# Loads of attention keys and queries issued by SyncE in place of GpSimd

## The chip, the cores and the metric

One core of a Trainium2 chip runs the whole program in one launch. The metric is the device time of one execution in microseconds (us). The engines are TensorE (PE, with its weight loads as PEld), VectorE (DVE), ScalarE (ACT), GpSimd (POOL) and SyncE (SP), each with its own queue of instructions, taken in order. A DMA is issued by an instruction in one of these queues and then runs on the core's 16 DMA engines.

## What is computed

The reference runs two transformer blocks over 1024 tokens of width 1024, in float32. The first has window attention, spatial gating, attention to a memory and a mixture of experts. The second has a recurrent unit beside a differential attention, and then experts that choose their tokens. The change lies in the differential attention of the second block: four heads, each with two sets of queries and keys of 64 channels and values of 128 channels.

```python
def diff_attention(q, k, v, g_q, g_k, lam, g_o, bias_table, lam_init):
    q = rms_norm_2(q, g_q) * (HEAD_DK ** -0.5)
    k = rms_norm_2(k, g_k)
    ...
    def block(args):
        ...
        s = jnp.einsum('bqhjd,bkhjd->bhjqk', qi, k).astype(jnp.float32) + bias[None, :, None]
        p = jax.nn.softmax(s, axis=-1)
        w = (p[:, :, 0] - lam * p[:, :, 1]).astype(v.dtype)
        return jnp.einsum('bhqk,bkhd->bqhd', w, v)
    ...
    o = rms_norm_2(o, g_o) * (1.0 - lam_init)
    return o.reshape(B, S, D_ATT)

def second_block(...):
    ...
        y_att = diff_attention(...)
        mix = jnp.dot(jnp.concatenate([y_lru, y_att], axis=-1), w_out[l])
        x = x + gate1 * mix
        h2 = rms_norm_2(x, g_norm2[l]) * (1.0 + scale2) + shift2
        x = x + gate2 * expert_choice_ffn(h2, w_router[l], w1[l], w3[l], w2[l])
```

## The kernel before

Matrix products work on pairs of tiles: an upper part (12 bits of the significand) and a lower part of each number, so that a product is made of several passes. Queries and keys are normed, split into both parts, transposed and stored in DRAM as `qT_d` and `kT_d`. Of the 128 rows of a tile there, 64 hold the upper parts of a head's 64 channels and 64 the lower ones.

`head_load` brings a head into nine SBUF tiles of 128 partitions by 1024 float32 numbers (512 KB each), with the tag `hd`. For each of the two sets there is a query tile `q` (upper rows on partitions 0 to 63, lower ones on 64 to 127) and two key tiles: `kh`, the upper key rows twice over the partitions, and `kl`, the lower key rows twice. Two strips `st` from `F_d` hold the position bias, and one tile holds the values from `v_d`. In the kernel before, queries (L2068) and keys (L2072) are issued from the GpSimd queue. The key load reads 64 rows through an access pattern whose outermost dimension repeats them twice. Strips (L2078) and values (L2084) are issued from the SyncE queue. There are slots for two heads (18 tiles of class `hd`).

For each head and each of 8 tiles of 128 queries, `diff_att` makes the scores of both sets on the PE (`diff_half`, L2108 with `kh` and L2109 with `kl`, into the PSUM tile `p_sc`), adds the bias and takes the minimum on DVE (L2115), takes exponents on ACT (L2098), combines the two sets (L2145 on DVE, or L2148 on ACT with L2150 on GpSimd), transposes the weights on the PE (L312, `p_wt`), copies them (L315 on ACT or L317 on DVE), multiplies them with the values (L2159, `p_o`), and norms the result with a power on GpSimd (L2166), after which it is transposed once more (L2175, `p_ot`).

The order on every queue is written when the program is built, by a list scheduler (`Sched`): generators yield pieces of work with an engine and an estimated cost, and the scheduler puts each at the end of its engine's queue in the order of the estimated times. A transfer is estimated on a virtual engine called DMA or, if GpSimd issues it, on POOL. Each engine then takes its queue in order, and an instruction waits by semaphores for the data and the buffers that it needs. A tile's buffer is one of 48 (`u`), taken over from some earlier tile, whose last reader must be done.

Around the head loads the same queues hold: on SyncE the stores of the values (`v_d<-v`), the output weights (`wraw<-in_w_out`, L369), the rows `gmod`, `grow` and `mscale`, and the other half of the mixed features (`yl<-ylru_d`); on GpSimd the products of the output weights with a gate row (L379, `wraw<-wraw,grow`).

After the attention come the output projection with the router (`out2`), the choice of each expert's tokens (`top_part`, `route2`) and 16 experts (`expert2`), whose weights stream from DRAM.

Of the kernel before, what the change touches and what calls it, by code (L numbers as in the profile page):

```python
# [37 lines left out]
# ---------------------------------------------------------------- order of the work  # L38

class Ev:  # L40
    """Something that a generator makes and others wait for."""
# [6 lines left out]
class Sched:  # L48
    """Puts the work of generators in one order for the engines' queues.

    A generator yields, before each piece of work, the engine that it keeps and an estimate of its
    time; the order is that of a list schedule by these estimates."""
# [17 lines left out]
    def spawn(self, prio, gen, at=0.0):  # L70
        g = [prio, self.n, gen, at, at, None, 0.0]   # prio, id, gen, ready, last, request, slots ready
        self.n += 1
        self.gens.append(g)
        cur = getattr(self, "cur", None)
        self._next(g, None)
        self.cur = cur
        return g
# [8 lines left out]
    # requests  # L86
# [9 lines left out]
    def give(self, cls, t=None, n=1):  # L96
        """Slots of a class back, from the end of the caller's last piece of work."""
# [87 lines left out]
# ---------------------------------------------------------------- pieces  # L185
# [26 lines left out]
def bcast_rows(ap, n, p=128):  # L212
    """A row of n values of DRAM on p partitions."""
    return bass.AP(tensor=ap.tensor, offset=ap.offset, ap=[[0, p], [1, n]])


class K:
# [15 lines left out]
    # pieces of generators  # L233
    def load(self, out, src, mb, eng=None):
        """A transfer of mb megabytes into out."""
# [7 lines left out]
    def split(self, hi, lo, src, n):  # L243
        """hi = the upper 12 bits of src's significand, lo = the rest."""
# [6 lines left out]
    def rstd(self, ss, n, mul=1.0):  # L251
        """mul / sqrt(ss / n + eps); mul is a power of two."""
        nc, S = self.nc, self.S
        w = ss.shape[1]
# [8 lines left out]
    def transposes(self, name, parts, outs, n=128):  # L263
        """Up to four [128, 128] blocks through one bank, then its upper and lower parts."""
# [12 lines left out]
    def tsplit(self, name, groups, view=lambda p: p):  # L277
        """Blocks transposed to both parts: groups of (parts, upper, lower, time from which the parts are there)."""
# [22 lines left out]
    def tcopy(self, name, groups, view=lambda p: p):  # L301
        """Blocks transposed: groups of (parts, output, time from which the parts are there)."""
# [23 lines left out]
    def gemm(self, out, hT, ch, n, whole=False):  # L326
        """out [128 tokens, n] = h @ W from upper and lower parts; hT(k) gives those of h."""
# [17 lines left out]
    def wload(self, chunks):  # L345
        """Streams chunks (weights, first column, columns, uses) of [K, columns] as both parts."""
        S, nc = self.S, self.nc
        pool = 0
        for n, ch in enumerate(chunks):
# [6 lines left out]
            if isinstance(ch, tuple):  # L356
                # these after what the gpsimd queue has by then
# [35 lines left out]
    def wdone(self, ch, i):  # L393
        """A user has read a piece of a chunk."""
# [4 lines left out]
    def short(self):  # L399
        """A small vector instruction, and the wait for what it wrote."""  # L400
        return self.S.op("DVE", 0.085, lat=0.01)
# [17 lines left out]
def staggered(pairs):  # L419
    """Each expert's last weights after the next expert's first ones."""  # L420
# [16 lines left out]
def gain_tile(k, name, src, n=1024):  # L437
    """A gain on all partitions."""
# [5 lines left out]
# ---------------------------------------------------------------- first block: mixers  # L444
# [23 lines left out]
def sgu_prep(k, ev):  # L468
    """Masked, transposed mixing weights [j, g, i] in both parts and the bias [i, g]."""
# [51 lines left out]
def sgu_mix(k, ghl, prep_ev, dones, s_ev):  # L521
    """s[t] = mixed gate + bias, token-major."""
# [50 lines left out]
def att_kv(k, t, hT, ch, gk, kT, vhl, done):  # L573
    """Keys: both parts, each twice over the partitions; values."""
# [35 lines left out]
def att_q(k, t, hT, ch, out_ev):  # L610
    """Normed queries, both parts on the partitions: [part * 64 + d, head, token]."""
# [32 lines left out]
def att_half(k, t, g, qT, at, kT, vhl, mask, nsink, sink, ev):  # L644
    """Four heads of a token tile: at[:, 4g:4g+4]."""
# [90 lines left out]
def out1(k, t, hT, chs, x_in, x1_d, gate, stored):  # L736
    """x1 = x + mixed @ w_out to DRAM."""
# [30 lines left out]
def proj_res(k, t, n, hT, ch, x_ev, done):  # L768
    """x[:, half n] += h @ W."""
# [26 lines left out]
def cross_norm(k, t, gate, x1_d, gain_ev, out_ev):  # L796
    """The norm of x1, transposed."""
# [155 lines left out]
def out_cross(k, t, o_ev, chs, x1_d, x2_d, h_d, gain_ev, wr_ev, lg, done, stored):  # L953
    """x2 = x1 + o @ w_co; it and its norm to DRAM; router logits."""
# [62 lines left out]
def first_mixers(k, x_in, x1_d, x2_d, h_d, sg_d, lg, moe=True, more=()):  # L1017
# [6 lines left out]
    # constants  # L1024
# [36 lines left out]
    def body():  # L1061
        """Everything in the order of its priority."""
# [18 lines left out]
        # spatial gating  # L1081
# [20 lines left out]
        # window attention  # L1102
# [40 lines left out]
        # memory  # L1143
# [60 lines left out]
        def load_wr():  # L1204
# [6 lines left out]
            # the norm's gain, by channel  # L1211
# [57 lines left out]
def grow(k, dones, tab):  # L1269
    """More slots for the experts' weights as the tokens' are given back."""  # L1270
# [12 lines left out]
def first_max(k, x, w, oh, mx, t):  # L1283
    """mx = max of x [128, w]; oh = 1 at its first place."""
# [11 lines left out]
def route_tile(k, t, lg, lgd, prev, done, gdone):  # L1296
    """Group and experts of a tile's tokens; their places in the table of the experts' slots."""
# [58 lines left out]
def route_gate(k, t, G, ohg, mg, m, c1, OH, lh, rh, gdone):  # L1356
    """Gates of both experts, with the group's weight."""
# [34 lines left out]
def tokens(k, tok, ids, q):  # L1392
    """Rows to gather; that of an empty slot is past every array."""
# [24 lines left out]
def route1_rest(k, dones, ev):  # L1418
    """Blocks of 128 past the first of each expert: where they start, and their slots."""
# [26 lines left out]
    # a slot of a first block is in no column  # L1446
# [30 lines left out]
def rest_place(k, evs, stop, cont):  # L1477
    """Stops the order of the work where the loop over the further blocks stands."""
# [13 lines left out]
def moe1_start(k, dones):  # L1492
    """Tiles that the tokens' rows are gathered into: empty slots keep what was there."""
# [80 lines left out]
def moe1_consts(k):  # L1574
# [5 lines left out]
    # tri[i, j] = 1 where i < j  # L1580
# [21 lines left out]
def moe1_rest(k, a, h_d, x_d):  # L1602
    """Experts with more than 128 tokens: their further blocks, one at a time."""
    nc, tc, cp = k.nc, k.tc, k.cp
    # expert of block j: the number of experts whose blocks end at or before j
# [62 lines left out]
# ---------------------------------------------------------------- second block  # L1668

def mod_vec(k, mod_d, ev):  # L1670
    """silu(c) @ w_mod + b_mod as a row in DRAM."""
# [38 lines left out]
def mod_gain(k, ev, gate, mod_d, j, g):  # L1710
    """g * (1 + scale) on all partitions."""
# [20 lines left out]
def second_norm(k, t, gate, x_d, g_ev, s_ev, hT2, out_ev):  # L1732
    """h1 transposed."""
# [971 lines left out]
```

## Time and profile before

| What | Value |
|---|---|
| median of 3 runs | 2645.89 us |
| lowest and highest run | 2645.14 and 2654.83 us |
| profiled execution, first to last instruction (its span) | 2648.8 us |
| profiled execution, time around its span | not shown |
| PE busy | 2403.0 us (91%) |
| DVE busy | 1961.7 us (74%) |
| ACT busy | 1574.9 us (59%) |
| GpSimd busy | 503.1 us (19%) |
| moved by DMA | 600.76 MB, 227 GB/s over the span |

Busy shares are averages over the whole span; stages differ, and what a change in one stage is worth is read from that stage. Times in the rows are counted from the span's start. The profile does not count the issue of a DMA as busy time of an engine.

### The profile page before, as it was taken

What the parts mean: (1) busy time and instruction counts of PE and PEld (TensorE: products, weight loads), DVE (VectorE), ACT (ScalarE), POOL (GpSimd) and SP (SyncE); (2) the same over time, 40 slices, a digit from 0 to 9 for tenths busy, and PEclk for the clock granted to TensorE, in tenths of its full rate; (3) what the DMA queues carried; (4) which work ended last, traced back from release to release, by engine and by line L of the source; (5) the groups of instructions that cost most, each with busy time, mean ns of one, the idle gap of its engine ahead of it and who ended that gap; (6) DMA issues with size and microseconds to landing.
All of it is one profiled execution on the core that took longest, in us unless ns stands there. A gap on an engine that the chain in (4) does not pass through costs nothing. (4 is left out here: it accounts for less than half of the span.)

```text
span 2648.8 us, 34944 instructions
## 1 busy us (share of the span) xinstructions
PE 2403.0 (91%) x11984; PEld 1975.1 (75%) x11984; DVE 1961.7 (74%) x3174; ACT 1574.9 (59%) x2419; POOL 503.1 (19%) x407
## 2 busy tenths in 40 slices
PE   7999999999698999999969998976894799999998
PEld 6887877888577877777747777765783688877776
DVE  6668457555788888888865546667829799899897
ACT  5357235442276877777864667655622577677775
POOL 1021011000321132111122202234435000110110
PEclk9999999999899999999979999988997899999999
DMA  4433465134688999999972213654326699999998
GB/s 152 149 111 124 166 232 203 47 112 152 205 271 290 344 302 322 348 341 345 350 263 81 79 53 108 154 115 112 103 104 246 225 359 358 380 374 373 375 373 270
DMA packets 328660, 600.76 MB, mean 227 GB/s; under 512 B 47176, under 2 KB 78476, under 8 KB 328480
## 3 DMA queue, kind: packets, MB, share of 16 engines
q1 hardware_dynamic: 296224, 550.15, 59.1%
q0 software_dynamic: 32256, 48.35, 7.6%
q8 instruction: 95, 1.56, 0.3%
q14 instruction: 85, 0.70, 0.1%
HBM read 554.25 MB, written 60.87 MB: 232 GB/s over the span
## 5 line engine op out<-in xcount | busy, mean ns | idle before, releaser
L389 DVE TENSOR_TENSOR wl<-wraw,wh 128x1024 fp32r<-128x1024 f32 x829 | 990.1, 1237 | 132.6 <-ACT wh L384 124.8
L384 ACT ACTIVATE wh<-wraw 128x1024 fp32r<-128x1024 f32 x852 | 846.0, 1051 | 90.7 <-DMA wraw<-in_w_ck_dram 34.8
L260 POOL TENSOR_TENSOR rs_r<-rs_v,mhalf 128x1 f32<-128x1 f32 (+2 forms) x111 | 103.7, 937 | 786.4 <-DVE rs_v L257 786.3
L340 PE MATMUL p_b<-wl,xT_h 128*128 128x512 f32 x512 | 203.0, 397 | 9.1 <-DVE wl L389 9.1
L340 PE MATMUL p_a<-wl,xT_h 128*128 128x512 f32 x512 | 204.4, 399 | 6.3 <-DVE wl L389 6.0
L339 PE MATMUL p_b<-wh,xT_h 128*128 128x512 f32 x512 | 205.3, 401 | 1.6 <-ACT wh L384 1.6
L339 PE MATMUL p_a<-wh,xT_h 128*128 128x512 f32 x512 | 206.2, 403 | 0.0
L341 PE MATMUL p_a<-wh,xT_l 128*128 128x512 f32 x512 | 201.5, 394 | 0.2 <-DVE xT_l L249 0.2
L341 PE MATMUL p_b<-wh,xT_l 128*128 128x512 f32 x512 | 201.0, 393 | 0.0
L339 PE MATMUL p_g<-wh,aT_h 128*128 128x512 f32 x384 | 157.5, 410 | 0.0
L341 PE MATMUL p_g<-wh,aT_l 128*128 128x512 f32 x384 | 150.8, 393 | 0.0
L340 PE MATMUL p_g<-wl,aT_h 128*128 128x512 f32 x384 | 150.7, 392 | 0.0
L1559 POOL DMA_INDIRECT x_d<-y,tok x32 | 60.0, 1873 | 351.7 <-ACT y L1550 348.0
L340 PEld LDWEIGHTS p_a<-wl,xT_h 128*128 128x128 f32 x512 | 97.1, 190 | 37.4 <-DVE wl L389 19.1
L2399 POOL DMA_INDIRECT out_dram<-y,tok x16 | 38.0, 2378 | 452.7 <-DVE y L2389 347.7
L340 PEld LDWEIGHTS p_b<-wl,xT_h 128*128 128x128 f32 x512 | 96.7, 189 | 35.6 <-DVE wl L389 16.9
L247 ACT ACTIVATE xT_h<-p_t 128x512 fp32r<-128x512 f32 x96 | 56.8, 596 | 95.8 <-PE p_t L269 95.3
L339 PEld LDWEIGHTS p_b<-wh,xT_h 128*128 128x128 f32 x512 | 96.8, 189 | 21.1 <-ACT wh L384 1.9
L341 PEld LDWEIGHTS p_a<-wh,xT_l 128*128 128x128 f32 x512 | 96.8, 189 | 20.2 <-DVE xT_l L249 0.6
L339 PEld LDWEIGHTS p_a<-wh,xT_h 128*128 128x128 f32 x512 | 97.2, 190 | 19.1
L341 PEld LDWEIGHTS p_b<-wh,xT_l 128*128 128x128 f32 x512 | 96.5, 188 | 19.8
L339 PE MATMUL p_y<-wh,hidT 128*128 128x512 f32 x256 | 103.6, 405 | 6.1 <-SPq L1624 6.1
(502 smaller groups left out, 5826.5 us busy)
## 6 DMA issues: line engine op xcount, KB each, us to landing
wraw<-in_w_dram SPq DMA_DIRECT2D x768, 512.0 KB
mraw<-in_w_mod_dram SPq DMA_DIRECT2D x48, 512.0 KB
x<-x_d SPq DMA_DIRECT2D x32, 512.0 KB
wraw<-in_w_in_dram SPq DMA_DIRECT2D x28, 512.0 KB
wraw<-in_w_out_dram SPq DMA_DIRECT2D x16, 512.0 KB
hd<-kT_d POOLq DMA_DIRECT2D x16, 512.0 KB, 20.2
x<-in_x_dram SPq DMA_DIRECT2D x8, 512.0 KB
xres<-in_x_dram SPq DMA_DIRECT2D x8, 512.0 KB
```

What stands on the lines that cost most here:

```text
L247: nc.scalar.activation(hi, src, AF.Copy)
L260: nc.gpsimd.tensor_tensor(r, v, self.mhalf[:, :w], op=OP.pow)
L339: nc.tensor.matmul(out, hh(k), wh, start=(k == 0), stop=False)
L340: nc.tensor.matmul(out, hh(k), wl, start=False, stop=False)
L341: nc.tensor.matmul(out, hl(k), wh, start=False, stop=(k == KK - 1))
L384: nc.scalar.activation(hi, raw, AF.Copy)
L389: (nc.vector if S.chosen == "DVE" else nc.gpsimd).tensor_tensor(lo, raw, f(hi), op=OP.subtract)
L1559: nc.gpsimd.indirect_dma_start(out=x_d, out_offset=bass.IndirectOffsetOnAxis(ap=k.tok[:, e:e + 1], axis=0), in_=y, in_offset=None, compute ...
L2399: nc.gpsimd.indirect_dma_start(out=out, out_offset=bass.IndirectOffsetOnAxis(ap=k.tok2[:, e:e + 1], axis=0), in_=y, in_offset=None, comput ...
```

## The change

Queries and keys are issued from the SyncE queue. A key tile is loaded by two transfers, one for each half of the partitions, both from the same 64 rows, in place of one that repeats the rows. The destination is viewed as plain float32 (`f(q)`, `f(kt)`). The scheduler's estimates change with it: 1.0 on POOL for each load becomes 1.5 on DMA for a query tile and 0.75 on DMA for half a key tile. The rest of the difference takes out comments and docstrings.

```diff
@@ -2064,17 +2064,17 @@
     for b in range(2):
         g = 2 * h + b
         q, kh, kl = hd[3 * b:3 * b + 3]
-        yield S.op("POOL", 1.0, after=[t0])
-        nc.gpsimd.dma_start(q, qT_d[g])
+        yield S.op("DMA", 1.5, after=[t0])
+        nc.sync.dma_start(f(q), qT_d[g])
         for kt, r in ((kh, 0), (kl, 64)):
-            src = kT_d[g, r:r + 64]
-            yield S.op("POOL", 1.0, after=[t0])
-            nc.gpsimd.dma_start(kt, bass.AP(tensor=src.tensor, offset=src.offset, ap=[[0, 2], [1024, 64], [1, 1024]]))
+            for o in (0, 64):
+                yield S.op("DMA", 0.75, after=[t0])
+                nc.sync.dma_start(f(kt)[o:o + 64], kT_d[g, r:r + 64])
         T["q", b], T["kh", b], T["kl", b] = q, kh, kl
```

The order of the instructions changes in the attention stage on all engines; behind it only buffer numbers differ on the PE. Two places matter for what follows.

The first is SyncE's queue where the third head (head 2) is loaded. `hd_16185` to `hd_16187` before, and `hd_16174` to `hd_16182` in the change, are its tiles. Before:

```order
L2084 DMA hd_15240<-v_d 128x1024
L2084 DMA hd_15454<-v_d 128x1024
L2078 DMA hd_16185<-F_d 128x1024
L2078 DMA hd_16186<-F_d 128x1024
L2084 DMA hd_16187<-v_d 128x1024
L369 DMA wraw<-in_w_out_dram 128x2x512 x2
L237 DMA gmod<-in_g_norm_2_dram 128x1024
```

With the change:

```order
L2084 DMA hd_15458<-v_d 128x1024
L2068 DMA hd_16174<-qT_d 128x1024
L2072 DMA hd_16175<-kT_d 64x1024 x2
L2072 DMA hd_16176<-kT_d 64x1024 x2
L2068 DMA hd_16177<-qT_d 128x1024
L2072 DMA hd_16178<-kT_d 64x1024 x2
L2072 DMA hd_16179<-kT_d 64x1024 x2
L2078 DMA hd_16180<-F_d 128x1024
L2078 DMA hd_16181<-F_d 128x1024
L2084 DMA hd_16182<-v_d 128x1024
L369 DMA wraw<-in_w_out_dram 128x2x512 x2
L2068 DMA hd_16721<-qT_d 128x1024
```

The ten loads of queries and half keys now stand between the last load of head 1 and the strips of head 2; head 3's loads (from `hd_16721`) follow the two loads of output weights, ahead of `gmod`.

The second is GpSimd's queue where the first products L379 stand. `r` is the power of a tile, `s` the sum of its two sets, `hd` tiles are head 3's. Before:

```order
L2166 TENSOR_TENSOR r_16779<-v_16778,mhalf 128x1
L2150 TENSOR_TENSOR s_16460<-s_16460,s_16461 128x512
L2072 DMA hd_16721<-kT_d 128x1x1024
L2068 DMA hd_16722<-qT_d 128x1024
L379 TENSOR_TENSOR wraw<-wraw,grow 128x1024 x4
L2166 TENSOR_TENSOR r_16863<-v_16862,mhalf 128x1
L2166 TENSOR_TENSOR r_16928<-v_16927,mhalf 128x1
L2072 DMA hd_16723<-kT_d 128x1x1024
```

With the change:

```order
L2166 TENSOR_TENSOR r_17026<-v_17025,mhalf 128x1
L379 TENSOR_TENSOR wraw<-wraw,grow 128x1024 x2
L2166 TENSOR_TENSOR r_17090<-v_17089,mhalf 128x1
L2150 TENSOR_TENSOR s_16668<-s_16668,s_16669 128x512
...
L2166 TENSOR_TENSOR r_17364<-v_17363,mhalf 128x1
L2150 TENSOR_TENSOR s_16981<-s_16981,s_16982 128x512
L379 TENSOR_TENSOR wraw<-wraw,grow 128x1024 x2
L2166 TENSOR_TENSOR r_17451<-v_17450,mhalf 128x1
```

The issues of loads are gone from this queue, and the four products stand in two pairs: one late among head 2's tiles, one among head 3's.

## Rows read from the trace of the kernel before

**Rows 1.** Span of the core and mean granted TensorE clock.

```profile
core 0: 2648.8 us, clock 0.959
```

**Rows 2.** Stretches: from:to, length; busy us (instructions) by engine; PEclk, DMA share, GB/s.

```profile
core 0: us, PE busy (x) PEld busy (x) DVE busy (x) ACT busy (x) POOL busy (x), PEclk, DMA share, GB/s
1720.00:1755.00 35.00, 34.63 (x244) 30.91 (x242) 34.80 (x121) 31.24 (x71) 18.09 (x21) 1.00 0.54 115
1755.00:1783.00 28.00, 9.85 (x32) 7.46 (x33) 5.94 (x21) 4.65 (x11) 3.14 (x4) 0.57 0.64 142
1783.00:1803.00 20.00, 20.00 (x142) 18.07 (x141) 18.05 (x62) 17.32 (x40) 10.46 (x13) 1.00 0.28 84
...
1813.00:1832.00 19.00, 15.30 (x95) 13.03 (x95) 18.96 (x56) 16.17 (x34) 7.04 (x8) 0.91 0.46 128
1832.00:1852.00 20.00, 8.45 (x36) 6.83 (x35) 7.05 (x19) 4.06 (x8) 1.83 (x3) 0.66 0.29 84
1852.00:1884.00 32.00, 31.12 (x216) 27.08 (x214) 29.75 (x101) 29.43 (x64) 11.40 (x12) 1.00 0.16 50
1884.00:1902.00 18.00, 12.85 (x93) 11.79 (x94) 10.00 (x23) 9.28 (x25) 7.46 (x7) 0.91 0.75 250
1905.00:2010.00 105.00, 100.94 (x528) 84.31 (x528) 52.01 (x101) 32.26 (x47) 45.52 (x24) 1.00 0.29 105
...
2075.00:2645.00 570.00, 559.50 (x2543) 452.48 (x2541) 511.36 (x500) 412.23 (x469) 56.86 (x29) 1.00 1.01 355
```

**Rows 3.** PE in order of time: start, us, instruction, [idle before <-releaser].

```profile
1680.01 0.39 PE L2108 MATMUL p_sc<-hd,hd 128*128 128x512 f32 x1
...
1760.86 0.77 PE L2108 MATMUL p_sc<-hd,hd 128*128 128x512 f32 x1 [5.93 <-DMA hd<-kT_d]
1771.19 0.80 PE L2109 MATMUL p_sc<-hd,hd 128*128 128x512 f32 x1 [9.56 <-DMA hd<-kT_d]
...
1842.07 0.77 PE L2108 MATMUL p_sc<-hd,hd 128*128 128x512 f32 x1 [9.68 <-DMA hd<-kT_d]
```

**Rows 4.** GpSimd in order of time, 1640 to 1920.

```profile
1649.84 0.61 POOL L2068 DMA_DIRECT2D hd<-qT_d  x1 [12.43 <-DMA qT_d<-qkT]
...
1734.50 0.63 POOL L2068 DMA_DIRECT2D hd<-qT_d  x1
...
1744.19 1.62 POOL L2072 DMA_DIRECT2D hd<-kT_d  x2
...
1803.42 9.25 POOL L379 TENSOR_TENSOR wraw<-wraw,grow 128x1024 f32<-128x1024 f32 x4
...
1828.77 0.84 POOL L2072 DMA_DIRECT2D hd<-kT_d  x1
```

**Rows 5.** SyncE's issues in order of time, 1600 to 1960.

```profile
1672.68 8.52 SPq L241 DMA_DIRECT2D v_d<-v  x3
...
1692.24 0.79 SPq L2084 DMA_DIRECT2D hd<-v_d  x2
1719.18 1.00 SPq L2078 DMA_DIRECT2D hd<-F_d  x2
...
1805.27 9.74 SPq L2078 DMA_DIRECT2D hd<-F_d  x2
...
1827.79 25.63 SPq L237 DMA_DIRECT2D yl<-ylru_d  x4
```

**Rows 6.** Line L2072, the key loads: from issue to landing.

```profile
DMA to landing us min/median/max: 15.9/20.2/31.3
```

**Rows 7.** DMA queues from 1836 to 1842, then 1720 to 1725: packets, MB, share of 16 engines.

```profile
q0 software_dynamic: 238, 0.43, 21.4%
...
q1 hardware_dynamic: 384, 1.44, 93.2%
```

**Rows 8.** DVE in order of time, 1798 to 1818.

```profile
1802.60 10.63 DVE L2145 SCALAR_TENSOR_TENSOR s<-s,c,s 128x512 f32<-128x512 f32 x1
```

**Rows 9.** DVE's groups, 1680 to 1902: busy us, mean ns | idle before.

```profile
L2145 DVE SCALAR_TENSOR_TENSOR s<-s,c,s 128x512 f32<-128x512 f32 x32 | 33.8, 1064 | 0.0
L317 DVE COPY wT<-p_wt 128x512 f32<-128x512 f32 x19 | 12.9, 682 | 1.2 <-PE p_wt L312 1.2
```

## Prediction

> **What bounds the kernel now.** I read the page first, then the table of stages, then the waits and the order in time of the attention stage. The page's busy shares are averages over stages with different limits; the change touches one stage, the attention of the second block, from about 1680 to 1902 us. The table of stages [rows 2] shows what the reader must see there. From 1720 to 1755 DVE is busy 34.80 of 35 us and the PE 34.63: the two engines together set the pace of a head, about 37.5 us (two heads' scores from 1680.01 [rows 3] to 1755). Then come two holes. From 1755 to 1783 DVE works 5.94 us of 28, from 1832 to 1852 it works 7.05 of 20, and the PE's granted clock falls to 0.57 and 0.66, near its 1.2 GHz level, after the engine had stood still. The PE in order of time says what ended the holes [rows 3]: 5.93 and 9.56 us before the first scores of head 2, and 9.68 us before a score of head 3, all waiting for `hd<-kT_d`, a key tile. Head 0 has no such wait: its first score, at 1680.01, carries no idle time before it, and the stretch to 1755 has none worth the name.
>
> Why are the keys late? GpSimd issues head 2's first query load at 1734.50 and its last pair of keys at 1744.19 [rows 4], while SyncE had issued the same head's bias strips at 1719.18 [rows 5]. So buffers were free some 15 us earlier; the loads stood in the GpSimd queue behind the additions L2150 and the powers L2166. Head 3's last key load leaves at 1828.77, behind the four products of L379, which take 9.25 us [rows 4]. And a key load is slow once issued: 15.9, 20.2 and 31.3 us to landing (least, median, most) [rows 6]. While hardly anything but two key loads is in flight, from 1836 to 1842 us, the GpSimd queue keeps 21.4% of the 16 DMA engines busy and moves 0.43 MB in 6 us, 72 GB/s; SyncE's strips and values move 1.44 MB in 5 us, 288 GB/s [rows 7]. 21.4% of 16 is 3.4 engines, so under two for each of the transfers.
>
> The Trainium skill, page "DMA: Bandwidth & Descriptors", section "Rules for kernel authors", says that a leading zero-stride broadcast of c copies holds a DMA to at most c engines; the old key load has c = 2, and the trace agrees (3.4 engines for two).
>
> **The change part by part.**
> *Removed from GpSimd:* 24 issues, 0.63 us for a query tile and 0.81 to 0.84 us for a key tile [rows 4], some 18 us. GpSimd is busy 18.09 of 35 us where the stage is full [rows 2], so I count nothing for it; what it hides behind are the scores on PE and DVE.
> *Added on SyncE:* 8 query loads and 32 half key loads, 0.4 to 0.5 us of issue each by the rows of the strips and values, where two take 1.00 and 0.79 us [rows 5], so 16 to 20 us in all. SyncE waits most of this stage. Cost: nothing, as long as nothing urgent stands behind a waiting load.
> *When the loads start.* The first group of order rows shows head 2's ten loads directly behind head 1's last one. By the program's semaphores its keys and queries wait for nothing later than the last score of head 0, and its strips and values for products a few tiles behind. The strips' issue at 1719.18 [rows 5] is the row nearest to that; ten issues from there end by about 1725. Head 3's loads follow behind two loads of output weights; their buffers come free from the end of head 1 (about 1755) to a third of the way into head 2.
> *How long they take.* A head is nine tiles of 0.524 MB, 4.72 MB. At 288 GB/s that is 16.4 us. No row shows a transfer of 64 partitions, so I bound it: not faster than 288 GB/s, and not slower than the old key loads' 72 GB/s. I take 288, the row of the same queue with the same 4 KB runs. Head 2 is then there by 1742, and its scores are wanted at 1755; head 3, if all nine tiles had to wait until 1768, by 1785, wanted at 1755 + 37.5 = 1792. Head 0 (from 1650, as on GpSimd now [rows 4]) is there by 1667, wanted at 1680. Head 1's loads stand behind the last store of values, issued by 1681.2, and most of them behind a wait for those stores to land, which ended at 1692.24 [rows 5]: there by 1709, wanted at 1680 + 37.5 = 1717.
>
> The page "SBUF — State Buffer" of the Trainium skill, section "Can I just issue two DMAs to hit both halves?", speaks against the halves: only a transfer over all 128 partitions reaches all ports, and two halves run one after the other. By it (an estimate) the keys would move at half of 288 GB/s, 14.6 us for 2.1 MB, and a head would take 23.7 us instead of 16.4; no run here shows it, and head 0 would still be there by 1674.
>
> *The sum.* The two holes: 28 + 20 = 48 us, in which 12.99 us of DVE work is done. In the four full stretches (1720 to 1755, 1783 to 1803, 1813 to 1832, 1852 to 1884) DVE is idle 4.44 of 106 us, 4.2% [rows 2], so that work takes 13.6 us without the wait: 34.4 us are freed. The slow clock after each hole is inside this figure.
> The scheduler also moves five copies of transposed weights (L317) from ACT to DVE: 5 x 0.68 us [rows 9] = 3.4 us, with DVE the bound.
> The products of L379 hold DVE: one L2145 ran from 1802.60 for 10.63 us while they ran [rows 8], against 0.75 us for the other 31 ((33.8 - 10.63) / 31) [rows 9]. The second group of order rows shows them split in two pairs. Bounds: the pairs hold DVE as the four did (no difference), or not at all (9.9 us gained). I take the first, since the same instruction still runs beside them.
> Saving: 34.4 - 3.4 = 31.0 us. What follows the stage (output projection to 2010, choice of tokens to 2075, experts to 2645) stands in the same order on the PE, and from 1905 to 2010 the DMA is busy 0.29 [rows 2]: the stream of expert weights waits there for buffers, not for bandwidth, so it starts earlier when the buffers do. I count no loss.
> The profiled execution's span is 2648.8 us [rows 1]; its time around the span is not shown. The median of the runs is 2645.9, 2.9 below. I take the saving from the median: 2645.9 - 31.0 = 2614.9, say **2615 us** (the span about 2618). No change can be told from one of 0.5%, 13 us.
>
> **Rivals.**
> *Head 3 is still late* because its buffers, not its queue, come late. For it: now the strips of head 3 leave only at 1805.27 on SyncE, which does not wait for GpSimd's queue [rows 5]. Against it: those stood behind DVE's 10.63 us. Then only the first hole closes: 28 - 5.94/0.958 - 3.4 = 18.4 us, 2627.5 us.
> *A new wait on GpSimd.* The second pair of L379 needs output weights whose load now stands on SyncE behind the four `yl` loads, and behind that pair on GpSimd wait powers and additions of head 3. In the trace those `yl` loads took SyncE 25.63 us from first to last, waiting for buffers [rows 5]. If all of that falls on the path, 31.0 - 25.6 = 5.4 us are left: 2640.5 us. Against it: the buffers they wait for are freed by tiles of the end of head 2, which are past before that pair's turn.
> *Slower: the half loads are slow.* If on one queue they run at the old keys' 72 GB/s, a head takes 65.6 us, the fourth is there at 1650 + 4 x 65.6 = 1912, and with 37.5 us for its scores and 18 of drain [rows 2] the stage ends at 1968 instead of 1902: 2712 us. It decides from 49 us for a head, 96 GB/s. Against it: the strips' 288 GB/s on that queue.
> *The gain is not handed on:* the experts' stage has the DMA at 1.01 of its time [rows 2]; were its stream tied to something other than the buffers of the stages before, the time would stay at 2646. Against it: the DMA's 0.29 before it.
>
> **How the numbers follow.** Both holes close: 0.72 (2615, own range 2603 to 2624: the holes without any idle and part of the 9.9 us, or 4 to 9 us of small new waits). Head 3 late: 0.12. New wait on GpSimd: 0.06. Not handed on: 0.05. Half loads slow: 0.05. The range takes the first two, 0.84: up to 2628 for head 3 late, and down to 2600 for both holes with all of the 9.9 us and a little less idle. Faster 0.84, same 0.11 (GpSimd's wait, not handed on), slower 0.05.
>
> **What would show it.** Right: no score waits for `hd<-kT_d` or `hd<-qT_d`; the keys of heads 2 and 3 are issued by SyncE by about 1725 and 1770; the granted clock stays near 1.00 from 1720 to the stage's end; the drain, which began at 1884 [rows 2], begins near 1853; the stages behind keep their lengths. Wrong: scores that still wait for key tiles, GpSimd's additions behind L379 waiting for `in_w_out`, or a stage from 1905 on that is longer by what attention gave.

## The result and the profile after

The changed kernel takes 2614.49 us (median of 4 runs, 2611.75 to 2616.46), the kernel before, beside it, 2646.64 us. The ratio is 0.9873 with a 95% interval of 0.9857 to 0.9888: 32 us less. The forecast was 2615 us. A repeat of the changed kernel, further down, has one run in a slower state of the chip, 3067.7 us at a granted clock of 0.74; it is left out of that ratio, and its profile is not used.

In the profiled execution [rows 1] becomes:

```profile
core 0: 2609.7 us, clock 0.966
```

The spans differ by 39.1 us, more than the medians, and only a part of that belongs to the change. Measured from the first score to the end of the last `p_ot` on the PE, the attention stage lasts from 1674.93 to 1858.65, 183.7 us, where it lasted 222.0 before (1680.01 to 1901.99): 38.3 us less. The first score is 5.1 us earlier in this execution; the PE makes the same 7750 matmuls ahead of it, and in the profiles of all the kernels below it falls between 1675 and 1681 us, so this is spread between executions. Behind the stage 751.0 us follow where 746.8 did, 4.2 us more. So the change accounts for about 38.3 - 4.2 = 34.1 us in these two profiles.

The table of stages, from:to, length, busy us of PE, PEld, DVE, ACT and POOL with instructions, granted clock, DMA share, GB/s. It answers to [rows 2]:

```profile
1715.00:1750.00 35.00, 34.09 (x230) 29.90 (x229) 34.24 (x113) 28.51 (x64) 12.64 (x14) 1.00 0.41 119
1750.00:1788.00 38.00, 37.81 (x275) 34.24 (x275) 36.51 (x126) 32.78 (x76) 14.73 (x17) 1.00 0.61 168
1788.00:1803.00 15.00, 11.37 (x58) 8.61 (x57) 15.00 (x41) 9.55 (x20) 7.47 (x5) 0.85 0.26 85
1803.00:1824.00 21.00, 19.96 (x134) 17.77 (x133) 19.03 (x58) 16.44 (x38) 8.25 (x8) 0.94 0.29 92
...
1861.00:1966.00 105.00, 100.08 (x522) 83.47 (x520) 51.78 (x96) 31.56 (x45) 43.15 (x23) 1.00 0.29 105
2031.00:2601.00 570.00, 561.91 (x2555) 455.29 (x2553) 512.91 (x502) 414.92 (x472) 57.88 (x29) 1.00 1.00 355
```

Both holes are gone: DVE is busy in 34.24 of 35 us and in 36.51 of 38, where the first hole had 5.94 of 28 [rows 2]; the second hole had 7.05 of 20, and no stretch here comes near that before the drain. What is left of low PE time, 11.37 of 15 us from 1788, has DVE full; it is the first pair of L379 (below).

On the PE, in order of time, the first scores of heads 2 and 3 carry no idle time, and no later score waits for keys, where scores of these heads in [rows 3] had 5.93, 9.56 and 9.68 us waiting for `hd<-kT_d`:

```profile
1748.80 0.40 PE L2108 MATMUL p_sc<-hd,hd 128*128 128x512 f32 x1
...
1788.55 0.48 PE L2108 MATMUL p_sc<-hd,hd 128*128 128x512 f32 x1
```

SyncE's queue in order of time (start, us, issue), the loads of heads 2 and 3, which answer to [rows 4, 5]:

```profile
1706.03 0.32 SPq L2068 DMA_DIRECT2D hd<-qT_d  x1
1706.44 2.88 SPq L2072 DMA_DIRECT2D hd<-kT_d  x4
1710.83 0.33 SPq L2068 DMA_DIRECT2D hd<-qT_d  x1
1712.18 2.37 SPq L2072 DMA_DIRECT2D hd<-kT_d  x4
...
1747.00 0.34 SPq L2068 DMA_DIRECT2D hd<-qT_d  x1
1748.52 2.56 SPq L2072 DMA_DIRECT2D hd<-kT_d  x4
...
1755.79 2.36 SPq L2072 DMA_DIRECT2D hd<-kT_d  x4
```

Head 2's keys are out by 1714.6, 34 us before the first of its scores; head 3's by 1758.2, 30 us before. And a load is short. Line L2072, from issue to landing, against 15.9, 20.2 and 31.3 us in [rows 6]:

```profile
DMA to landing us min/median/max: 3.7/5.5/7.3
```

The trace after the change can't say by itself which of the two did it, the queue or the shape of the load. The experiments can.

### The profile page after: what moved, and what is told of

Its sections match the earlier page's. It is cut to its first block, busy times and chain, and to the rows that moved or that the text cites. A ratio compares the mean times of both kernels' runs of the same rounds, so it can differ in the third digit from the quotient of the medians.

```text
span 2609.7 us, 34986 instructions
## 1 busy us (share of the span) xinstructions
PE 2396.9 (92%) x11984; PEld 1973.6 (76%) x11984; DVE 1964.9 (75%) x3179; ACT 1573.1 (60%) x2414; POOL 484.5 (19%) x383
## 5 line engine op out<-in xcount | busy, mean ns | idle before, releaser
L389 DVE TENSOR_TENSOR wl<-wraw,wh 128x1024 fp32r<-128x1024 f32 x829 | 992.9, 1241 | 128.9 <-ACT wh L384 118.4
L384 ACT ACTIVATE wh<-wraw 128x1024 fp32r<-128x1024 f32 x852 | 846.1, 1051 | 89.3 <-DMA wraw<-in_w_ck_dram 34.4
L341 PEld LDWEIGHTS p_a<-wh,xT_l 128*128 128x128 f32 x512 | 96.8, 189 | 20.2 <-DVE xT_l L249 0.6
L340 PE MATMUL p_y<-wl,hidT 128*128 128x512 f32 x256 | 103.9, 406 | 4.6 <-DVE wl L389 4.3
```

The lines of the kernel that those rows point to most:

```text
L340: nc.tensor.matmul(out, hh(k), wl, start=False, stop=False)
L341: nc.tensor.matmul(out, hl(k), wh, start=False, stop=(k == KK - 1))
L384: nc.scalar.activation(hi, raw, AF.Copy)
L389: (nc.vector if S.chosen == "DVE" else nc.gpsimd).tensor_tensor(lo, raw, f(hi), op=OP.subtract)
```

## The experiments

The gain has two candidate causes, and the prediction used both: the keys stood in GpSimd's queue (late), and the load that repeats its rows holds few DMA engines (slow). The first two experiments make one part of the change each. The table gives each run's ratio to the kernel before, timed beside it, with the length of the attention stage in its profile, from first score to last `p_ot`. There is one profile of each kernel, so a difference of 2 or 3 us between two stages may be no more than spread (below, the spare transfers). Where an edit adds a line, the lines behind it move by one or two in the rows: scores L2108 and L2109 become L2109 and L2110, key loads L2073 or L2074.

| Kernel | us | ratio and interval | stage, us |
|---|---|---|---|
| changed | 2614.5 | 0.9873 (0.9857 to 0.9888) | 183.7 |
| repeating load on SyncE | 2687.6 | 1.0158 (1.0141 to 1.0176) | 254.2 |
| halves on GpSimd | 2611.8 | 0.9875 (0.9858 to 0.9891) | 186.3 |
| changed loads, order of before | 2616.3 | 0.9888 (0.9869 to 0.9908) | 186.2 |
| each half twice | 2661.1 | 1.0064 (1.0047 to 1.0081) | 226.8 |
| repetition behind the rows | 2607.2 | 0.9854 (0.9835 to 0.9873) | 179.4 |
| a second transfer beside each half | 2616.1 | 0.9877 (0.9860 to 0.9895) | 186.6 |
| one transfer for a key tile | 2608.3 | one run | 179.4 |
| gate behind the product | 2603.8 | 0.9831 (0.9813 to 0.9849) | 175.6 |
| repetition behind the rows, gate behind | 2601.0 | 0.9812 (0.9798 to 0.9826) | 172.4 |
| changed, once more | 2620.6 | 0.9890 (0.9875 to 0.9905) | not read |

**The queue alone.**

```diff
-            for o in (0, 64):
-                yield S.op("DMA", 0.75, after=[t0])
-                nc.sync.dma_start(f(kt)[o:o + 64], kT_d[g, r:r + 64])
+            src = kT_d[g, r:r + 64]
+            for o in (0, 64):
+                yield S.op("DMA", 0.75, after=[t0])
+            nc.sync.dma_start(f(kt), bass.AP(tensor=src.tensor, offset=src.offset, ap=[[0, 2], [1024, 64], [1, 1024]]))
```

> Issued by SyncE in the order of the changed kernel, but each key tile again by one load that repeats its 64 rows. My theory (the keys were late mostly because of where they stood in GpSimd's queue, and slow besides): the loads leave at the times of the changed kernel (head 2 by 1715, head 3 by 1758), land after the 16 to 31 us that the old loads took, so by about 1746 and 1789, where their scores are wanted at 1749 and 1788: 2612 to 2625 us. Rival, the repeating pattern alone made the holes: 2632 to 2646. If repeating loads run one after the other on this queue at 20 us each, a head takes 80 us: above 2700.

It is 1.6% slower than the kernel before. The PE in order of time, scores of all four heads, waits for keys (last figures: idle before, and its releaser):

```profile
1688.74 0.76 PE L2109 MATMUL p_sc<-hd,hd 128*128 128x512 f32 x1 [6.90 <-DMA hd<-kT_d]
1698.61 0.79 PE L2110 MATMUL p_sc<-hd,hd 128*128 128x512 f32 x1 [9.11 <-DMA hd<-kT_d]
...
1756.32 0.80 PE L2110 MATMUL p_sc<-hd,hd 128*128 128x512 f32 x1 [10.53 <-DMA hd<-kT_d]
...
1809.02 0.80 PE L2110 MATMUL p_sc<-hd,hd 128*128 128x512 f32 x1 [10.59 <-DMA hd<-kT_d]
...
1865.61 0.79 PE L2110 MATMUL p_sc<-hd,hd 128*128 128x512 f32 x1 [13.02 <-DMA hd<-kT_d]
```

The DMA queues of the same run from 1724 to 1735, a stretch in the middle of a head's loads (packets, MB, share of 16 engines), and two rows of SyncE's queue:

```profile
q1 hardware_dynamic: 143, 0.57, 12.8%
```

```profile
1722.54 18.64 SPq L2079 DMA_DIRECT2D hd<-F_d  x2
...
1803.35 10.12 SPq L2073 DMA_DIRECT2D hd<-kT_d  x2
```

12.8% of 16 is 2.0 engines, and 0.57 MB in 11 us is 52 GB/s. SyncE's loads go one behind the other, and it takes 18.64 us to issue two strips that took 1.00 us before [rows 5], 17.3 of them in one issue instruction: a slow load holds back what stands behind it on its queue, also loads that use all engines. The loads of head 2 begin at 1743.33 and those of head 3 at 1800.01, 57 us apart. That is the mechanism of the prediction's rival "the half loads are slow", which decides from 49 us for a head; only it is the old load that is slow on this queue. My expectation that these loads would be nearly in time fell: its theory left out that they run one at a time. The last case that I named, loads one after the other, is what happened, with 57 us for a head where I put 80, and so with 2687.6 us and not above 2700.

**The shape alone.**

```diff
-            nc.gpsimd.dma_start(kt, bass.AP(tensor=src.tensor, offset=src.offset, ap=[[0, 2], [1024, 64], [1, 1024]]))
+            for o in (0, 64):
+                nc.gpsimd.dma_start(kt[o:o + 64], src)
```

> Issued by GpSimd in the order of the kernel before, but each key tile by two loads of 64 partitions. My theory: head 2's keys still leave at 1735 to 1747, but land in about 5 us and so by 1752, before they are wanted at 1755: the first hole (21.8 us) closes; head 3's still stand behind the four products of L379, so about half of the second hole's 12.6 us stays: 2614 to 2628 us. Rival, the place in the queue alone made the holes: 2636 to 2646.

The whole gain is there without moving anything: 2611.8 us, below the 2614 to 2628 that I expected, since the half of the second hole that I left standing closed as well. GpSimd in order of time, heads 2 and 3, and the landing time of its key loads:

```profile
1737.29 2.10 POOL L2073 DMA_DIRECT2D hd<-kT_d  x4
...
1741.86 2.07 POOL L2073 DMA_DIRECT2D hd<-kT_d  x4
...
1778.36 9.24 POOL L379 TENSOR_TENSOR wraw<-wraw,grow 128x1024 f32<-128x1024 f32 x4
...
1798.13 1.09 POOL L2073 DMA_DIRECT2D hd<-kT_d  x2
```

```profile
DMA to landing us min/median/max: 3.4/6.2/11.1
```

The keys stand where they stood in [rows 4], half of head 3's behind the products of L379, but with 3 to 11 us to land no score waits over 1 us for them. The queue alone is not the cause, in either direction: late and short is early enough, early and slow is not.

**The order of the other engines.** The changed loads on SyncE, with the estimates of before, so that PE, DVE, ACT and the rest of GpSimd keep the order of before.

```diff
-        yield S.op("DMA", 1.5, after=[t0])
+        yield S.op("POOL", 1.0, after=[t0])
         nc.sync.dma_start(f(q), qT_d[g])
         for kt, r in ((kh, 0), (kl, 64)):
+            yield S.op("POOL", 1.0, after=[t0])
             for o in (0, 64):
-                yield S.op("DMA", 0.75, after=[t0])
                 nc.sync.dma_start(f(kt)[o:o + 64], kT_d[g, r:r + 64])
```

> The changed loads, with the scheduler's estimates of before, so that PE, DVE and ACT have the order of before: five L317 copies back on ACT (3.4 us less on DVE), the four products of L379 in one piece (9.9 us of hold on DVE instead of the 6.2 that I count in the changed trace). My theory (the order is worth nothing by itself): 2610 to 2619 us. Rival, the order carries a part of the gain: above 2624.

2616.3 us, as expected, and not to be told from the changed kernel. Its stage, 186.2 us, equals that of the halves on GpSimd, 186.3, which has the same order on PE, DVE and ACT: in sum the two queues make no difference once the load is short. The parts differ. With the halves on GpSimd one combination of the two sets (L2145, there L2146) beside the four products of L379 takes 10.88 us, much as in [rows 8]; here three DVE instructions beside the same four products take 2.30, 1.93 and 1.70 us, an excess of 4.8 us in place of 10.1. This run loses time elsewhere, in head 0: with the wait below and a granted clock of 0.50 to 0.55 for the 12 us around it, head 1 begins 43.4 us behind head 0, where it is 38.7 with the halves on GpSimd. That the sums meet is partly chance. Against the changed kernel's 183.7 the stage is 2.5 us longer; of the order that shows nothing, as a kernel below in the changed order has 186.6. One wait of this run shows what may stand behind loads on SyncE: head 0's values left at 1687.99 only, with those of head 1, and the first `p_o` waited for them:

```profile
1698.50 6.41 PE L2159 MATMUL p_o<-hd,wT 128*128 128x128 f32 x32 [2.85 <-DMA hd<-v_d]
```

**How much slack the loads have.** First each half load issued twice into the same place:

```diff
                 nc.sync.dma_start(f(kt)[o:o + 64], kT_d[g, r:r + 64])
+                nc.sync.dma_start(f(kt)[o:o + 64], kT_d[g, r:r + 64])
```

> Each half key load issued twice, so a head is 6.8 MB instead of 4.7: at 288 GB/s 23.7 us for a head. My theory (the loads have slack): heads 2 and 3 are still there before they are wanted, no score waits for keys: 2611 to 2619 us. Rival, the loads are at the edge of being late: 4 to 8 us for each of heads 1 to 3, 2625 us and more.

2661.1 us: it came out slower than before, and as the rival wanted it, but the trace shows another reason. SyncE, two halves in a row:

```profile
1770.63 0.44 SPq L2073 DMA_DIRECT2D hd<-kT_d  x1
1771.13 0.59 SPq L2072 DMA_DIRECT2D hd<-kT_d  x1
1775.01 0.45 SPq L2073 DMA_DIRECT2D hd<-kT_d  x1
1775.50 0.60 SPq L2072 DMA_DIRECT2D hd<-kT_d  x1
```

The second load (L2073) writes what the first one (L2072) writes, so by the program's semaphores it waits until that has landed: some 4 us each time, 32 times, in a queue on which everything else stands behind. The experiment tested that wait and not the bytes. So the same bytes went into a place of their own, in DRAM (`k.spare`, 32 tiles of 64 by 1024 numbers, read by nobody):

```diff
                 nc.sync.dma_start(f(kt)[o:o + 64], kT_d[g, r:r + 64])
+                nc.sync.dma_start(k.spare[4 * g + r // 32 + o // 64], kT_d[g, r:r + 64])
```

> Beside each half key load a second transfer of the same rows, into its own place in DRAM that nothing reads, so that no load waits for another as in the run with every half issued twice; the bytes are the same, 6.8 MB a head. Theory: the loads have slack and that run lost its time to 32 waits of about 4 us on SyncE's queue: 2611 to 2620 us, no score waits for a key. Rival, the loads are at the edge of being late: 2625 us and more.

2616.1 us, as expected, and no score waits for a key: 2.1 MB more for each head cost nothing that the times can show. (They go to DRAM, so nothing is said of more bytes into SBUF.) The stage is 2.9 us longer than the changed kernel's in the profiles, but the first score of head 3 comes 113.2 us behind that of head 0 here and 113.6 there, so the extra time lies in head 3's own tiles and the drain, behind all the loads.

**What makes the load slow.** One load that repeats its rows, with the repetition inside instead of outermost; the query tile is interleaved alike.

```diff
-        nc.sync.dma_start(f(q), qT_d[g])
+        src = qT_d[g]
+        nc.sync.dma_start(f(q), bass.AP(tensor=src.tensor, offset=src.offset, ap=[[1024, 64], [65536, 2], [1, 1024]]))
...
-                nc.sync.dma_start(f(kt)[o:o + 64], kT_d[g, r:r + 64])
+            nc.sync.dma_start(f(kt), bass.AP(tensor=src.tensor, offset=src.offset, ap=[[1024, 64], [0, 2], [1, 1024]]))
```

> SyncE, the changed kernel's order, and one load for a key tile that repeats its rows, but with the repetition behind the rows: row i goes to partitions 2i and 2i + 1 (the query tile is loaded with upper and lower rows interleaved in the same way, so the scores are the same sums). Theory after the first four runs: it is the repetition as the outermost dimension that holds a load to two engines. Then these land in about the halves' 4 to 7 us, with all 16 engines busy, and the time is 2609 to 2620 us. Rival, a load that repeats rows is slow wherever the repetition stands: 15 us and more to landing, 2670 to 2690 us as with the outermost repetition on this queue.

2607.2 us, a little under the 2609 to 2620 that I expected; its interval overlaps the changed kernel's. The landing of its key loads (L2074), and its DMA queue from 1706 to 1708, while keys and queries are in flight:

```profile
DMA to landing us min/median/max: 4.4/5.2/7.0
```

```profile
DMA packets 221, 0.81 MB, mean 406 GB/s; under 512 B 23, under 2 KB 23, under 8 KB 221
...
q1 hardware_dynamic: 221, 0.81, 101.8%
```

The same bytes, repeated just so, on the same queue: 16 engines instead of two, 406 GB/s instead of 52. Not the repetition but its place in the access pattern made the load slow. By the Trainium skill, page "DMA: Bandwidth & Descriptors", section "Rules for kernel authors", the outermost dimension sets how many engines a DMA gets, and one should be put there whose size is a multiple of 16; the trace agrees on both sides, 2.0 engines with the 2 outermost, 16 with the 64.

**What halves cost.** One transfer of 128 different rows in place of two halves.

```diff
             for o in (0, 64):
                 yield S.op("DMA", 0.75, after=[t0])
-                nc.sync.dma_start(f(kt)[o:o + 64], kT_d[g, r:r + 64])
+            nc.sync.dma_start(f(kt), kT_d[g])
```

> One load over all 128 partitions in place of the two halves (a key tile then holds upper and lower rows, not the same ones twice, so these scores are other numbers). It measures what halves cost: in the changed trace, while keys and queries alone are in flight, 1710 to 1714, the queue moves 0.46 MB in 2 us. If halves run at half the rate, about 1 MB in 2 us here for the keys; if they run nearly as fast as whole tiles, 0.5 to 0.6 MB in 2 us. I expect the second, and a time within 6 us of the changed kernel's.

The DMA of the changed kernel from 1710 to 1714, and of this one from 1706 to 1710, both with only keys and queries in flight:

```profile
DMA packets 273, 0.92 MB, mean 230 GB/s; under 512 B 48, under 2 KB 48, under 8 KB 273
...
q1 hardware_dynamic: 273, 0.92, 103.3%
```

```profile
DMA packets 399, 1.47 MB, mean 368 GB/s; under 512 B 40, under 2 KB 40, under 8 KB 399
...
q1 hardware_dynamic: 399, 1.47, 91.3%
```

With all engines busy in both, mostly halves run at 230 GB/s and whole tiles at 368: 0.63 of the rate. It lies between my two answers. The time, from a single run, is 6.2 us below the changed kernel's, at the edge of the 6 that I allowed. In one place the rate shows, in the middle of head 0. Two windows of the changed kernel, then of the interleaved one, beginning some 9 and 15 us behind the first score of each:

```profile
1684.00:1690.00 6.00, 3.17 (x13) 1.36 (x11) 6.00 (x22) 5.38 (x10) 2.52 (x2) 0.94 1.04 246
1690.00:1696.00 6.00, 5.01 (x22) 4.64 (x23) 4.73 (x15) 2.60 (x5) 1.27 (x1) 0.50 1.03 285
```

```profile
1684.70:1690.70 6.00, 3.16 (x13) 1.41 (x12) 6.00 (x22) 5.33 (x10) 2.51 (x2) 1.00 1.03 417
1690.70:1696.70 6.00, 6.00 (x50) 5.63 (x51) 6.00 (x18) 4.66 (x10) 1.84 (x2) 1.00 0.34 135
```

The PE does the same little work in the first window of both, behind DVE. Then its clock stands at 0.50, the 1.2 GHz level, in the changed kernel, and at 1.00 in the other, and 22 matmuls are done against 50. Ahead of it the PE in order of time has one pause more in the changed kernel, 0.99 us before the first `p_o`, which the profile puts down to a copy on ACT. Again the changed kernel first, then the interleaved one:

```profile
1689.96 1.11 PE L312 MATMUL p_wt<-ident,s 128*128 128x128 f32 x4 [1.78 <-DVE s L2145]
1692.07 3.75 PE L2159 MATMUL p_o<-hd,wT 128*128 128x128 f32 x16 [0.99 <-ACT wT L315]
```

```profile
1690.60 0.66 PE L312 MATMUL p_wt<-ident,s 128*128 128x128 f32 x4 [1.78 <-DVE s L2147]
1691.10 2.01 PE L2161 MATMUL p_o<-hd,wT 128*128 128x128 f32 x16
```

The other kernels in the changed order divide in the same way. With halves (spare transfers, gate behind the product) the first `p_o` has a pause of 1.44 and 1.45 us before it and the 6 us around it a clock of 0.72 and 0.59; with whole tiles (one transfer, both improvements) there is neither. Both kernels with whole tiles and L379 have a stage of 179.4 us, 4.3 less than the changed one, and 3.1 of that is there when head 1 begins in the interleaved one (34.0 us behind head 0, against 37.1). That the pause is a wait for head 0's value tile, behind head 1's loads in a full DMA, is likely: the copy that the profile names had ended at 1689.97, 2.1 us before, and the run with the order of before names the tile. It is not shown.

**The products of L379.** Taken out; the gate row multiplies the product in PSUM instead, before it is added.

```diff
-    for ch in c["o"]:
-        ch.cols = gt1
...
-        yield S.op("DVE", t_dve(512))
+        G = yield S.wait(gt)
+        yield S.op("DVE", 2 * t_dve(512))
+        nc.vector.tensor_tensor(p, p, G[:, s], op=OP.mult)
         nc.vector.tensor_tensor(x[:, s], x[:, s], p, op=OP.add)
```

> The changed kernel with the products of L379 taken out: the gate row multiplies the output projection in PSUM on DVE instead (16 more DVE instructions of 0.7 us, 11 us, in a stage where DVE is busy 54 of 107). My theory: the 6.2 us by which the two pairs of L379 hold DVE in the attention stage come free, and the 5.4 us for which ACT waits for the last four: 2603 to 2610 us. Rivals: the holds lie beside other waits, 2611 to 2618; the added instruction delays the free banks of PSUM in the output projection, 2619 to 2626.

2603.8 us, as expected. The stage is 8.1 us shorter than the changed kernel's, and 747.1 us follow it instead of 751.0. Not all of the 8.1 need come from the holds: the order moves a little too, and DVE makes 20 of the copies L317 where the changed kernel has 24, 2.5 us less. What the products did there is seen in the changed kernel, GpSimd and DVE in order of time:

```profile
1790.20 4.72 POOL L379 TENSOR_TENSOR wraw<-wraw,grow 128x1024 f32<-128x1024 f32 x2
...
1825.57 5.17 POOL L379 TENSOR_TENSOR wraw<-wraw,grow 128x1024 f32<-128x1024 f32 x2
```

```profile
1791.21 1.39 DVE L2137 SCALAR_TENSOR_TENSOR c<-c,lam,den 128x1 f32<-128x1 f32 x1
1792.52 0.15 DVE L2138 SCALAR_TENSOR_TENSOR e<-den 128x1 f32<-128x1 f32 x1
1792.59 0.68 DVE L2115 CUSTOM_DVE_ANT_0 s<-p_sc,hd 128x512 f32<-128x512 f32 x1
...
1793.20 2.27 DVE L2145 SCALAR_TENSOR_TENSOR s<-s,c,s 128x512 f32<-128x512 f32 x1
```

L2145 takes 2.27 us, against 0.75 alone (worked out from [rows 9]), and L2137 1.39 for a column of one number; L2115, which reads the scores in PSUM, takes its 0.68 between them. The Trainium skill, page "SBUF — State Buffer", section "SBUF: two separate sides", has a pair of ports that DVE and GpSimd lock against each other for a whole instruction, on DVE's side also for one with two SBUF inputs beside a GpSimd operation that reads SBUF; the rows agree. With the second pair (2.28 and 1.45 us where 0.75 and 0.15 would do) the excess is 1.2 + 1.5 + 1.5 + 1.3 = 5.5 us. (The expectations put it at 6.2; an L2137 of 0.70 us at 1824.92 lies beside an addition L2150, not beside the pair, and is not counted here.)

**Both improvements together**, and the changed kernel once more beside it.

> Interleaved key and query tiles in one load each (as in the run with the repetition behind the rows) together with the gate row multiplied in behind the output projection in place of L379. If the two gains are apart, as I think (the stage's first head without the dip of the clock, 4 us; DVE's holds and the late start of the output projection, 10 us): 2597 to 2603 us. Rival, both work on the same slack of the stage: 2603 to 2608, no better than the gate alone.

> The changed kernel once more, with nothing changed in the program, on the chip and in the rounds of the run beside it, as the base for it: 2611 to 2617 us.

2601.0 us, as expected, ratio 0.9812, against 2620.6 and 0.9890 beside it (above the 2611 to 2617 that I expected of the repeat, with an interval that overlaps its first one): the best kernel here, faster than the changed one by 0.8%, with intervals apart. The two gains nearly add up in the profiles (a stage of 172.4 us, 11.3 less than the changed kernel's, where one gave 8.1 and the other 4.3); in the times, the step from the gate alone (0.9831) lies within the intervals.

## Why the prediction was right, step by step

**The sum.** 34.4 us from the two holes: confirmed in size by the halves on GpSimd, which keep the order of before and its long hold by L379, 222.0 - 186.3 = 35.7. The term of the copies (3.4 us lost on DVE) is there as work: the changed kernel has 24 of these copies for 19, 16.0 us for 12.9 [rows 9]. As loss it can't be seen, since the stage is shorter than expected and not longer; it is not excluded either. L379, taken as no difference, was mis-sized: its pairs hold DVE for 5.5 us, not the 9.9 of [rows 8, 9], and the bounds in the prediction were right. The prediction's 31.0 would have made a stage of 191.0 us; it is 183.7. The step that failed on the other side is "what follows: I count no loss": 4.2 us more in these profiles. The first gather of tokens for the experts comes 162.3 us behind the stage's end before and 164.8 us with the change, so 2.5 of the 4.2 are lost ahead of it. There, in the last tiles of the output projection, DVE's five L389 (the lower parts of the experts' first weights) take 9.4 us where they took 6.0, beside GpSimd's own products; that these holds are the 2.5 us is likely, and no run tests it. The cause of the rest, 1.7 us, is open. Median against median the saving is 32 us. So the total is nearer than its parts, and that is luck: errors of 7 and 4 us stand against each other.

**Why the keys were late.** This step is right in its facts and wrong in its weight. The prediction put the GpSimd queue first and counted on earlier issue; the halves on GpSimd, issued as late as before, give the same time. The gain of the holes comes from the load's shape. The two engines that the prediction read from [rows 7], and used for the landing time alone, were the cause, and the old load in SyncE's queue makes the kernel 1.6% slower.

**When the loads start.** Head 2's by about 1725 and head 3's by about 1770 were foreseen; 1714.6 and 1758.2 it is, in a trace that runs 5 us ahead. Head 0 had no wait for keys.

**How long they take.** 288 GB/s was taken for halves. Measured are 230 for mostly halves and 368 for whole tiles: my row (strips) was no measure for either. The Trainium skill's page "SBUF — State Buffer", section "Can I just issue two DMAs to hit both halves?", has the direction right; the factor is 0.63 here and not the half of the estimate. It was hidden for heads 1 to 3, as the spare transfers show, and probably cost some 3 to 4 us in head 0.

**SyncE's issues at nothing** held: no wait of over 1 us behind them in the changed kernel, with the 0.99 us before `p_o` as the open one. **GpSimd's issues at nothing** held too, as the halves on GpSimd show: 32 half issues there, no loss in the time. The profiles leave one question. There, as in the kernel before, the long-held instruction began some 1 us ahead of the products, while GpSimd issued loads, and lost 10.1 us; with the loads on SyncE in the same order three instructions lost 4.8 us beside the products. No run parts the issues from the products.

**The rivals.** Head 3 still late: no wait. The new wait on GpSimd: the second pair of L379 began at 1825.57, directly behind an addition (L2150) begun at 1824.34; it waited for nothing. Half loads slow: not the halves, but the repeating load on SyncE took that way and made 254.2 us of stage. Not handed on: refuted by the time.

**The signs.** No score waits for keys or queries, and the loads left in time. Two signs did not hold as written: the granted clock is 0.85 in the 15 us from 1788, where the first pair of L379 lies, and 0.94 in the 21 us behind them, and the stages after the attention are 4.2 us longer together.

## What to carry to other kernels

Read a slow load's share of the 16 DMA engines before blaming its queue: here 2 engines of 16 said it all, and the outermost dimension of the access pattern is the one to change. A queue move and a reshaped load in one change need two experiments, since here the one was worth nothing that the times show and, without the other, a loss. When an experiment adds a write to a place already being written, the order it forces is what one measures.

## What was not expected of the hardware

The same repeating load runs at 72 GB/s on GpSimd's queue, where two are in flight [rows 7], and at 52 GB/s on SyncE's, where they go one by one and hold back the issue of loads that need not wait for them (18.64 us for two strips). Mostly loads of 64 partitions reach 230 GB/s with all engines busy, those of 128 reach 368. The same four products of L379 held DVE for 10.1 us in one kernel and for 4.8 us in another with the same order on DVE. The granted clock can fall behind a short pause of the PE, and the same pause need not bring it down: behind 1.78 us without a matmul it fell in the changed kernel (0.77 from 1689.0 to 1689.5, 0.50 after that, so the four transposes took 1.11 us for 0.66), and stayed at 1.00 in the interleaved one. With the spare transfers it stayed at 1.00 behind 1.79 us and fell in the next pause, of 1.44 us.
